# Embedding squares summed in bursts of four tiles, and pool input columns accumulated onto banks that ScalarE has seeded

## The chip, the cores and the metric

The kernel runs on one core of a Trainium2 chip. The time is that of one execution on the device, in microseconds (us): before the change a median of 2209.13 over 3 runs (2203.75 to 2210.25). One further execution was profiled; it took 2208.09, and its span from the first to the last instruction is 2206.3. All times in the rows below are microseconds from the start of that span.

The engines are TensorE (PE; its weight loads are listed apart as PEld), VectorE (DVE), ScalarE (ACT), GpSimd (POOL) and SyncE (SP), which issues the DMAs.

## The reference, cut to what matters

```python
def trunk_layer(x, p, S0, buf0, start, w_in, w_pool, ...):      # two layers; 512 prompt + 64 sample tokens
    h = rmsnorm(x, pre_g)
    proj = h @ w_in
    u, gp, q, k, v, gr = jnp.split(proj, SPLITS, axis=-1)
    pool_y, buf_new = pool_mixer(u, buf0, start, w_pool, pool_scale)   # causal means of 2, 4, 8, 16 tokens
    pool_y = pool_y * jax.nn.silu(gp)
    ret_y, S_new = retention(q, k, v, S0, start)
    ret_y = head_rmsnorm(ret_y).reshape(B, L, RET_WIDTH) * jax.nn.silu(gr)
    mix = jnp.concatenate([pool_y, ret_y], axis=-1) @ w_out
    x = x + rmsnorm(mix, post_g)
    ple = rmsnorm(p @ w_ple, ple_g)
    gate = jax.nn.sigmoid(x @ w_ple_gate + b_ple_gate)
    return x + gate * ple, S_new, buf_new
```

`pool_mixer` takes four groups of 256 channels: a windowed sum over tokens, divided by the count, minus `u`, times a 256 x 256 matrix. The gain `pre_g` is multiplied into the input before the product with `w_in`; the root of the norm, one number per token, is multiplied in afterwards (`rB`).

## The kernel before

All activations are held transposed: 128 channels on the partitions, 576 tokens (512 prompt, 64 sample) along the free dimension, in two halves of 288 columns (`half`, `HN`), because one PSUM bank takes one half. An fp32 product is made of three passes: each operand is split into a rounded upper part and a rest (`split`, L88: a cast on ACT, a subtraction on DVE), and upper x upper, upper x rest and rest x upper are added up in PSUM.

Each of the two layers runs through these stages.

- `in_first` (L386): the first half of the input channels times `w_in`, by a scheme with seven products in place of eight (`unit`, L234). The partial results go to DRAM (`proj_dram`).
- `in_phase` (L469): the second half. `columns(pr)` (L472) gives two tiles of 128 output channels. For each it loads the partial result into a buffer of the tag `part` (L478), splits the weights, and calls `gemm` (L129): 8 x 3 passes x 2 halves = 48 matmuls of 288 columns into two banks of the tag `acc`. Then DVE adds bank and partial result into the `part` tile (L484). Four heads come first (queries, keys, values and a gate, eight columns each), then four pool groups, g = 3, 2, 1, 0.
- `pool_group(g)` (L656): two input columns. Each is multiplied by `rB` into a tile `e` of the tag `d` (L669, L670), and its sample part into a tile `es` of the tag `u` (L672), which is first filled from DRAM (L663). Two scans per column (L680) give the windowed sums, the second of the tiles `tmp` and `es`. L682 to L689 make the means, and the result is split into two `u` tiles. Then come two gate columns (L500, L501), and for each half of the group's output the product with `w_pool` into `po` banks (L696) and the product with the gate into a tile `y` of the tag `d` (L700, L704). Between the groups, `operands(..., tag="part")` prepares what `out_phase` needs.
- `out_phase` (L721): the output projection by units, its norm (`rsqrt` of `rM`, L749, with two squares into `tmp` at L748), then the per-layer embedding: for 16 tiles, L761 to L770, a `gemm` of 12 matmuls, the square of both banks on ACT (L766, L316), their copy into a `part` tile (L768), the sum of the square over channels by four small matmuls with a tile of ones (`token_sums`, L290 and L292; each shows as two instructions), and the store. All 16 sums add up in one `po` bank. Then the gate product, which starts from the mixed result and the norm `rM`.

The order of the instructions on each engine is made by a planner ahead of time: it goes through the program, and places each instruction where its own simulation finds the engine free and the inputs there. An instruction that first writes a tile also waits for a buffer of the tile's tag. The numbers of buffers per tag are in `BUFS` (L44): `part` 4, `tmp` 4, `d` 4, `u` 6, `g` 2; there are 4 `acc` banks (L121), 2 `po` (L124) and 2 `pb` (L127).

Of the kernel before, what the change touches and what calls it, by code (L numbers as in the profile page):

```python
# [11 lines left out]
ALU = mybir.AluOpType  # L12
# [4 lines left out]
KT = 16  # L17
# [16 lines left out]
def half(ap, h):  # L34
    return ap[:, h * HN:(h + 1) * HN]
# [3 lines left out]
def decoder_kernel(ctx: ExitStack, tc: tile.TileContext, a, decay8):  # L39
# [86 lines left out]
    def bank(shape):  # L126
        return ps.tile(list(shape), F32, tag="pb", name="pb", bufs=2)  # L127

    def gemm(w, xs, new=acc_tile, by_half=False):  # L129
        acc = [new()[:, :HN] for _ in range(2)]  # L130
        n = len(w)
        for hs in ((0,), (1,)) if by_half else ((0, 1),):
            for i, ((wh, wl), (xh, xl)) in enumerate(zip(w, xs)):
                for passno, (u, v) in enumerate(((wh, xh), (wh, xl), (wl, xh))):
                    for h in hs:
                        nc.tensor.matmul(  # L136
                            acc[h], u, v[:, h * HN:(h + 1) * HN],
                            start=(i == 0 and passno == 0), stop=(i == n - 1 and passno == 2),
                        )
        return acc  # L140

# [148 lines left out]
    def token_sums(sums, src, start, stop):  # L290
        for q in range(4):
            nc.tensor.matmul(sums[32 * q:32 * q + 32], ones, src[:, q * QN:(q + 1) * QN], start=start, stop=stop)  # L292

    def rsqrt(out, srcs, n, sums=None):
        if sums is None:
            sums = mix_tile()[:, :QN]
            for i, src in enumerate(srcs):
                token_sums(sums, src, i == 0, i == len(srcs) - 1)
        v, t, r = (w[:, i * QN:(i + 1) * QN] for w in (tmp(),) for i in range(3))
        nc.vector.tensor_scalar(v, sums, 1.0 / n, EPS, op0=ALU.mult, op1=ALU.add)  # L300
        nc.vector.tensor_scalar(r.bitcast(I32), v.bitcast(I32), 1, None, op0=ALU.logical_shift_right)
        nc.vector.tensor_scalar(r.bitcast(I32), r.bitcast(I32), -1.0, float(0x5F3759DF), op0=ALU.mult, op1=ALU.add)
        for _ in range(3):
            nc.vector.scalar_tensor_tensor(out=t, in0=r, scalar=-0.5, in1=r, op0=ALU.mult, op1=ALU.mult)
            nc.vector.tensor_tensor(out=t, in0=t, in1=v, op=ALU.mult)
            nc.vector.scalar_tensor_tensor(out=r, in0=t, scalar=1.5, in1=r, op0=ALU.add, op1=ALU.mult)
        for h in range(2):
            rows = mix_tile()[:, :HN]
            for q in (2 * h, 2 * h + 1):
                nc.tensor.matmul(rows[:, (q % 2) * QN:(q % 2 + 1) * QN], pick[:, q], r, start=True, stop=True)  # L310
            nc.scalar.copy(half(out, h), rows)

    def square(out, src):
        if isinstance(src, list):
            for h in range(2):
                nc.scalar.activation(half(out, h), src[h], AF.Square)  # L316
        else:
            nc.scalar.activation(out, src, AF.Square)

# [11 lines left out]
    def load_tables():  # L331
# [6 lines left out]
        consts["kdec_s"] = load_const("kdec_s", [P, NH, NS])  # L338
        consts["mask_s"] = load_const("mask_s", [P, NH, 64])
        consts["invcnt"] = load_const("invcnt", [P, 4, 16])  # L340

    def after_all(ins, others):
        for other in others:
            tc.add_manual_dep(
                ins.ins, other.ins.name, mybir.DependencyInfo(mybir.DependencyClass.Sync, mybir.DependencyReason.DATA),
                reason="one burst",
            )

    def retention_state(l, h, s0_ring, qrep, kst, vst, po_s):
        for bg in range(2):  # L350
# [118 lines left out]
    def in_phase(l, raws, r2, rB, cos, sin):  # L469
        b_ring, st_ring, rot_ring, s0_ring = Ring(0, 12), Ring(12, 4), Ring(16, 8), Ring(24, 4)  # L470

        def columns(pr):  # L472
            keys = [("in2", p) for p in pairs] + [("out", 0, 0), ("out", 0, 1)]
            i = keys.index(("in2", pr))
            raw = raws.pop(("in2", pr))
            for c in range(2):
# [2 lines left out]
                w = split_weights(raw, 8 * c, 8)  # L479
                if c == 1:  # L480
                    fetch(l, raws, keys[i + 1:i + 3])
                acc = gemm(w, r2)
                for h in range(2):
                    nc.vector.tensor_tensor(out=half(t, h), in0=acc[h], in1=half(t, h), op=ALU.add)  # L484
# [171 lines left out]
        def pool_group(g):  # L656
# [7 lines left out]
            wh, wl = buf("u", (P, 2, DK), F32R), buf("u", (P, 2, DK), F32R)  # L664
            split(wh, wl, wraw)
            xs = []
            for i, t in enumerate(columns(g)):
                e = buf("d", (P, 16 + NP))
                nc.vector.memset(e[:, :16], 0.0)  # L669
                nc.vector.tensor_tensor(out=e[:, 16:], in0=t[:, :NP], in1=rB[:, :NP], op=ALU.mult)  # L670
                seg = es[:, i, 16:].rearrange("p (b s) -> p b s", s=SEG)
                nc.vector.tensor_tensor(  # L672
                    out=seg[:, :, BUF:], in0=t[:, NP:].rearrange("p (b s) -> p b s", s=NS),
                    in1=rB[:, NP:].rearrange("p (b s) -> p b s", s=NS), op=ALU.mult,
                )
                nc.scalar.copy(npool[:, i, 0], e[:, NP + 1:])
# [44 lines left out]
    def out_phase(l, raws, ops_out):  # L721
# [30 lines left out]
        for k in range(2):  # L752
# [3 lines left out]
            split(hi, lo, t)  # L756
            pp.append((hi, lo))
        sums = mix_tile()[:, :QN]
        for c8 in range(2):
            raw = load_weights(a["w_ple"][l, :, c8 * 8:(c8 + 1) * 8].rearrange("p c k n -> p (c k) n"))  # L760
            w = split_weights(raw, 0, 16)  # L761
            for c in range(8):
                ct = c8 * 8 + c
                acc = gemm(w[2 * c:2 * c + 2], pp)
                t, sq = buf("part"), buf("u")
                square(sq, acc)  # L766
                for i in range(2):
                    nc.scalar.copy(half(t, i), acc[i])  # L768
                token_sums(sums, sq, ct == 0, ct == KT - 1)
                nc.sync.dma_start(out=ple_dram[l][ct], in_=t)  # L770

        def residual(first):
            def xs(k):
# [192 lines left out]
```

## Time and profile before

| | us |
|---|---|
| median of 3 runs | 2209.13 |
| lowest, highest | 2203.75, 2210.25 |
| the profiled execution | 2208.09 |
| its span | 2206.3 |

The page of the profile gives the busy time of each engine over the span, the costliest groups of instructions by line, and the chain of work that ended last. Matmuls are pipelined, so a matmul's own duration (some 290 ns) is longer than the distance from one start to the next (some 130 ns for 288 columns); stretches of many matmuls tell more than single durations. A line can be that of a helper: L316 is any square of two banks, L318 any other square, L91 any rest of a split. Numbers in brackets behind a row of a timeline are the engine's idle time before it, and what ended it.

### The profile page before, as it was taken

The page shows a single profiled execution, that of the slowest core. Times are in us where ns is not written, and L with a number is a line of the kernel's source. Part 1 is how long each engine was busy: PE and PEld are TensorE (multiplying, and loading weights), DVE is VectorE, ACT ScalarE, POOL GpSimd, SP SyncE. Part 2 cuts the span into 40 slices and gives each one's busy share as a digit, 9 for nine tenths or more (in the row PEclk, how much of TensorE's full clock was granted, in tenths as well). Part 3 has the DMA queues.
Part 4 walks back from the last instruction along what each step waited for, and adds up shares of the span by engine and source line. Part 5 has one row for each costly group of instructions (what it writes and reads, how often), then busy time and mean ns, then how long its engine had stood idle before and what let it go on. Part 6 is the DMA issues. An engine that isn't in the chain of part 4 may idle for free.

```text
span 2206.3 us, 42552 instructions
## 1 busy us (share of the span) xinstructions
PE 2179.7 (99%) x16692; PEld 2138.2 (97%) x16692; DVE 1724.1 (78%) x3186; ACT 1059.0 (48%) x2097; POOL 89.5 (4%) x65
## 2 busy tenths in 40 slices
PE   8999999999999999999999999999999999999998
PEld 8999999999999999899999999999999999998998
DVE  8788766767689998888877786666676899988865
ACT  5465433444334555655455554433343345566532
POOL 2000000000000110000110000000000011100000
PEclk9999999999999999999999999999999999999999
DMA  6454455546453434556644444455554543345554
GB/s 227 146 195 166 155 169 159 174 160 186 152 177 127 136 118 136 196 171 219 201 161 152 166 156 152 161 178 173 159 171 152 171 147 123 112 144 192 175 197 151
DMA packets 138729, 361.98 MB, mean 164 GB/s; under 512 B 14496, under 2 KB 52896, under 8 KB 117664
## 3 DMA queue, kind: packets, MB, share of 16 engines
q1 hardware_dynamic: 138528, 359.26, 49.3%
q8 instruction: 131, 2.15, 0.4%
q14 instruction: 70, 0.57, 0.1%
HBM read 273.17 MB, written 86.04 MB: 163 GB/s over the span
## 4 chain that ended last, share of the span: by engine, by line
PE 87%; DVE 5%; DMA 5%; issue 2%; ACT 1%; SPq 0%; POOL 0%; DVEq 0%; ACTq 0%; POOLq 0%
PE acc L136 32%; PE acc L118 12%; PE acc L117 12%; PE acc L116 12%; PE acc L226 4%; DMA x<-ple 3%; PE pb L116 3%; PE pb L117 3%; PE pb L118 3%; PE po L292 1%; PE po L136 1%; DVE wl L91 1%; DVE x L801 1%; PE po L359 1%; PE pb L375 1%
## 5 line engine op out<-in xcount | busy, mean ns | idle before, releaser
L136 PE MATMUL acc<-m,wh 128*128 128x288 f32 x3584 | 657.0, 297 | 4.0 <-DVE part L484 4.0
L90 ACT CAST wh<-raw 128x512 fp32r<-128x512 f32 x567 | 350.3, 619 | 530.3 <-PE acc L136 288.1
L117 PE MATMUL acc<-m,wh 128*128 128x288 f32 x1944 | 572.3, 295 | 0.0
L116 PE MATMUL acc<-m,wh 128*128 128x288 f32 x1944 | 570.4, 295 | 0.8 <-ACT m L249 0.8
L118 PE MATMUL acc<-m,wl 128*128 128x288 f32 x1944 | 566.3, 295 | 1.2 <-DVE wl L91 1.2
L136 PEld LDWEIGHTS acc<-m,wh 128*128 128x128 f32 x3584 | 534.7, 189 | 11.7 <-issue 8.4
L91 DVE TENSOR_TENSOR wl<-raw,wh 128x512 fp32r<-128x512 f32 x567 | 395.7, 700 | 130.1 <-ACT wh L90 122.7
L136 PE MATMUL acc<-m,wl 128*128 128x288 f32 x1792 | 396.9, 296 | 0.0
L116 PEld LDWEIGHTS acc<-m,wh 128*128 128x128 f32 x1944 | 364.3, 188 | 2.0 <-ACT m L249 1.5
L117 PEld LDWEIGHTS acc<-m,wh 128*128 128x128 f32 x1944 | 364.8, 188 | 0.0
L118 PEld LDWEIGHTS acc<-m,wl 128*128 128x128 f32 x1944 | 362.3, 188 | 2.1 <-DVE wl L91 2.1
L90 ACT CAST wh<-S 128x512 fp32r<-128x512 f32 x356 | 220.6, 620 | 252.8 <-PE acc L117 146.1
L136 PEld LDWEIGHTS acc<-m,wl 128*128 128x128 f32 x1792 | 292.6, 189 | 1.9 <-issue 1.4
L91 DVE TENSOR_TENSOR wl<-S,wh 128x512 fp32r<-128x512 f32 x356 | 250.8, 706 | 24.6 <-ACT wh L90 23.2
L239 POOL TENSOR_TENSOR S<-raw 128x512 f32<-128x512 f32 x45 | 71.4, 1588 | 1923.6 <-DMA raw<-in_w_out 664.9
L484 DVE TENSOR_TENSOR part<-acc,part 128x288 f32<-128x288 f32 x192 | 79.3, 451 | 69.8 <-PE acc L136 67.3
L239 DVE TENSOR_TENSOR S<-raw 128x512 f32<-128x512 f32 x133 | 94.8, 712 | 10.8 <-DMA raw<-in_w_in 7.4
L116 PE MATMUL pb<-m,wh 128*128 128x288 f32 x324 | 95.3, 294 | 0.6 <-ACT wh L90 0.6
L117 PE MATMUL pb<-m,wh 128*128 128x288 f32 x324 | 95.5, 295 | 0.0
L118 PE MATMUL pb<-m,wl 128*128 128x288 f32 x324 | 95.0, 293 | 0.0
L249 ACT COPY d<-acc 128x288 f32<-128x288 f32 x228 | 86.1, 394 | 0.0
L254 DVE TENSOR_TENSOR d<-d,acc 128x288 f32<-128x288 f32 x114 | 51.3, 450 | 39.6 <-PE acc L118 39.3
(264 smaller groups left out, 3289.6 us busy)
## 6 DMA issues: line engine op xcount, KB each, us to landing
raw<-in_w_in SPq DMA_DIRECT2D x95, 1024.0 KB, 5.3
raw<-in_w_out SPq DMA_DIRECT2D x32, 1024.0 KB, 4.8
raw<-in_w_gate SPq DMA_DIRECT2D x32, 1024.0 KB, 5.3
proj<-d SPq DMA_DIRECT2D x96, 288.0 KB, 2.2
part<-proj SPq DMA_DIRECT2D x96, 288.0 KB, 3.0
m<-in_state_ret SPq DMA_DIRECT2D x64, 256.0 KB, 3.3
out_new_ret_s<-m SPq DMA_DIRECT2D x64, 256.0 KB, 3.2
x<-m SPq DMA_DIRECT2D x48, 288.0 KB, 3.4
```

The costliest lines, as they stand in the source:

```text
L90: nc.scalar.copy(hi, src)
L91: return nc.vector.tensor_tensor(out=lo, in0=src, in1=hi.bitcast(F32), op=ALU.subtract)
L116: nc.tensor.matmul(out, wh, xh, start=start, stop=False, **kw)
L117: nc.tensor.matmul(out, wh, xl, start=False, stop=False, **kw)
L118: nc.tensor.matmul(out, wl, xh, start=False, stop=stop, **kw)
L136: nc.tensor.matmul(acc[h], u, v[:, h * HN:(h + 1) * HN], start=(i == 0 and passno == 0), stop=(i == n - 1 and passno == 2),)
L226: nc.tensor.matmul(acc[h], w[:, j], xs[h][passno == 1], start=(i == 0 and j == 0 and passno == 0), stop=(i == 1 and j == 3 and passno == 2),)
L239: eng.tensor_tensor(out=s, in0=x, in1=y, op=op)
L249: ops["tail_act"] = nc.scalar.copy(dst, src)
L254: return nc.vector.tensor_tensor(out=dst, in0=dst, in1=src, op=ALU.add)
L292: nc.tensor.matmul(sums[32 * q:32 * q + 32], ones, src[:, q * QN:(q + 1) * QN], start=start, stop=stop)
L484: nc.vector.tensor_tensor(out=half(t, h), in0=acc[h], in1=half(t, h), op=ALU.add)
```

## The change

Two changes are made at once.

First, the sums of the embedding's squares. `token_sums` was called for each of the 16 tiles. Now the squares are kept in a list, and when four are there, `together` issues the matmuls of all four; its first one waits in addition for the last square of the four (`last_square`, `after_all`). The square tiles, before in buffers of `u`, now take the tags tmp, tmp, tmp, tmp, g, g, u, u in turn.

Second, the pool group's input columns. `columns(g, seeded=True)` has ScalarE copy the two halves of the partial result from the `part` tile into the two `acc` banks before the first matmul (`seed`), and the matmuls add to it (`start` is false from the first one on). The DVE addition of L484 falls away for these 2 columns of 4 groups in 2 layers, and the generator hands out the two banks in place of the `part` tile. The product with `rB` reads the banks: it becomes two instructions, 288 and 224 columns wide, and the product for the sample part reads the second bank.

```diff
--- before.py
+++ after.py
@@ -126,16 +126,22 @@
     def bank(shape):
         return ps.tile(list(shape), F32, tag="pb", name="pb", bufs=2)
 
-    def gemm(w, xs, new=acc_tile, by_half=False):
+
+
+    def gemm(w, xs, new=acc_tile, by_half=False, seed=None):
         acc = [new()[:, :HN] for _ in range(2)]
         n = len(w)
+        if seed is not None:
+            for h in range(2):
+                nc.scalar.copy(acc[h], half(seed, h))
         for hs in ((0,), (1,)) if by_half else ((0, 1),):
             for i, ((wh, wl), (xh, xl)) in enumerate(zip(w, xs)):
                 for passno, (u, v) in enumerate(((wh, xh), (wh, xl), (wl, xh))):
                     for h in hs:
                         nc.tensor.matmul(
                             acc[h], u, v[:, h * HN:(h + 1) * HN],
-                            start=(i == 0 and passno == 0), stop=(i == n - 1 and passno == 2),
+                            start=(seed is None and i == 0 and passno == 0), stop=(i == n - 1 and passno == 2),
+                            skip_group_check=seed is not None,
                         )
         return acc
 
@@ -291,6 +297,16 @@
         for q in range(4):
             nc.tensor.matmul(sums[32 * q:32 * q + 32], ones, src[:, q * QN:(q + 1) * QN], start=start, stop=stop)
 
+    def together(sums, srcs, start, stop):
+        for i, src in enumerate(srcs):
+            for q in range(4):
+                mm = nc.tensor.matmul(
+                    sums[32 * q:32 * q + 32], ones, src[:, q * QN:(q + 1) * QN],
+                    start=start and i == 0, stop=stop and i == len(srcs) - 1,
+                )
+                if q == i == 0:
+                    after_all(mm, [last_square[0]])
+
     def rsqrt(out, srcs, n, sums=None):
         if sums is None:
             sums = mix_tile()[:, :QN]
@@ -310,10 +326,19 @@
                 nc.tensor.matmul(rows[:, (q % 2) * QN:(q % 2 + 1) * QN], pick[:, q], r, start=True, stop=True)
             nc.scalar.copy(half(out, h), rows)
 
+    last_square = [None]
+
+    def after_all(ins, others):
+        for other in others:
+            tc.add_manual_dep(
+                ins.ins, other.ins.name, mybir.DependencyInfo(mybir.DependencyClass.Sync, mybir.DependencyReason.DATA),
+                reason="one burst",
+            )
+
     def square(out, src):
         if isinstance(src, list):
             for h in range(2):
-                nc.scalar.activation(half(out, h), src[h], AF.Square)
+                last_square[0] = nc.scalar.activation(half(out, h), src[h], AF.Square)
         else:
             nc.scalar.activation(out, src, AF.Square)
 
@@ -338,13 +363,6 @@
         consts["kdec_s"] = load_const("kdec_s", [P, NH, NS])
         consts["mask_s"] = load_const("mask_s", [P, NH, 64])
         consts["invcnt"] = load_const("invcnt", [P, 4, 16])
-
-    def after_all(ins, others):
-        for other in others:
-            tc.add_manual_dep(
-                ins.ins, other.ins.name, mybir.DependencyInfo(mybir.DependencyClass.Sync, mybir.DependencyReason.DATA),
-                reason="one burst",
-            )
 
     def retention_state(l, h, s0_ring, qrep, kst, vst, po_s):
         for bg in range(2):
@@ -469,7 +487,7 @@
     def in_phase(l, raws, r2, rB, cos, sin):
         b_ring, st_ring, rot_ring, s0_ring = Ring(0, 12), Ring(12, 4), Ring(16, 8), Ring(24, 4)
 
-        def columns(pr):
+        def columns(pr, seeded=False):
             keys = [("in2", p) for p in pairs] + [("out", 0, 0), ("out", 0, 1)]
             i = keys.index(("in2", pr))
             raw = raws.pop(("in2", pr))
@@ -479,6 +497,9 @@
                 w = split_weights(raw, 8 * c, 8)
                 if c == 1:
                     fetch(l, raws, keys[i + 1:i + 3])
+                if seeded:
+                    yield gemm(w, r2, seed=t)
+                    continue
                 acc = gemm(w, r2)
                 for h in range(2):
                     nc.vector.tensor_tensor(out=half(t, h), in0=acc[h], in1=half(t, h), op=ALU.add)
@@ -664,13 +685,14 @@
             wh, wl = buf("u", (P, 2, DK), F32R), buf("u", (P, 2, DK), F32R)
             split(wh, wl, wraw)
             xs = []
-            for i, t in enumerate(columns(g)):
+            for i, acc in enumerate(columns(g, seeded=True)):
                 e = buf("d", (P, 16 + NP))
                 nc.vector.memset(e[:, :16], 0.0)
-                nc.vector.tensor_tensor(out=e[:, 16:], in0=t[:, :NP], in1=rB[:, :NP], op=ALU.mult)
+                nc.vector.tensor_tensor(out=e[:, 16:16 + HN], in0=acc[0], in1=rB[:, :HN], op=ALU.mult)
+                nc.vector.tensor_tensor(out=e[:, 16 + HN:], in0=acc[1][:, :NP - HN], in1=rB[:, HN:NP], op=ALU.mult)
                 seg = es[:, i, 16:].rearrange("p (b s) -> p b s", s=SEG)
                 nc.vector.tensor_tensor(
-                    out=seg[:, :, BUF:], in0=t[:, NP:].rearrange("p (b s) -> p b s", s=NS),
+                    out=seg[:, :, BUF:], in0=acc[1][:, NP - HN:].rearrange("p (b s) -> p b s", s=NS),
                     in1=rB[:, NP:].rearrange("p (b s) -> p b s", s=NS), op=ALU.mult,
                 )
                 nc.scalar.copy(npool[:, i, 0], e[:, NP + 1:])
@@ -756,18 +778,22 @@
             split(hi, lo, t)
             pp.append((hi, lo))
         sums = mix_tile()[:, :QN]
+        squares = []
         for c8 in range(2):
             raw = load_weights(a["w_ple"][l, :, c8 * 8:(c8 + 1) * 8].rearrange("p c k n -> p (c k) n"))
             w = split_weights(raw, 0, 16)
             for c in range(8):
                 ct = c8 * 8 + c
                 acc = gemm(w[2 * c:2 * c + 2], pp)
-                t, sq = buf("part"), buf("u")
+                t, sq = buf("part"), buf(("tmp", "tmp", "tmp", "tmp", "g", "g", "u", "u")[ct % 8])
                 square(sq, acc)
                 for i in range(2):
                     nc.scalar.copy(half(t, i), acc[i])
-                token_sums(sums, sq, ct == 0, ct == KT - 1)
                 nc.sync.dma_start(out=ple_dram[l][ct], in_=t)
+                squares.append(sq)
+                if len(squares) == 4:
+                    together(sums, squares, ct == 3, ct == KT - 1)
+                    squares = []
 
         def residual(first):
             def xs(k):
```

## Rows read from the trace of the kernel before

**Rows 1.** The page: busy time of the engines; two of its groups.
```profile
PE 2179.7 (99%) x16692; PEld 2138.2 (97%) x16692; DVE 1724.1 (78%) x3186; ACT 1059.0 (48%) x2097; POOL 89.5 (4%) x65
...
L484 DVE TENSOR_TENSOR part<-acc,part 128x288 f32<-128x288 f32 x192 | 79.3, 451 | 69.8 <-PE acc L136 67.3
...
L249 ACT COPY d<-acc 128x288 f32<-128x288 f32 x228 | 86.1, 394 | 0.0
```
**Rows 2.** The chain of waits, 876 to 894 us: start, us, what.
```profile
876.11 6.58 PE acc L136 x48
...
883.67 1.92 PE po L292 x56
...
887.37 0.38 PE po L292 x8
...
889.54 0.37 PE po L292 x4
...
892.63 0.98 PE acc L136 x6
```
**Rows 3.** Line L292 in the first layer's embedding: count, duration ns, first and last start.
```profile
L292 PE MATMUL po<-u,ones x128: 286/286/310, 883.7 to 912.4; 128*32 128x144 f32 x128
```
**Rows 4.** Timeline of PE behind the pool waits: start, us, what [idle before].
```profile
639.88 0.50 PE L136 MATMUL acc<-m,wh 128*128 128x288 f32 x2 [2.01 <-DVE part L484]
...
1733.98 0.50 PE L136 MATMUL acc<-m,wh 128*128 128x288 f32 x2 [2.01 <-DVE part L484]
```
**Rows 5.** Timeline of ACT, head 3's normaliser.
```profile
608.82 0.89 ACT L311 COPY tmp<-po 128x288 f32<-128x288 f32 x2 [0.28 <-PE po L310]
```
**Rows 6.** Timeline of DVE, first layer's pool stage, 565 to 633 us.
```profile
569.13 0.82 DVE L484 TENSOR_TENSOR part<-acc,part 128x288 f32<-128x288 f32 x2
...
570.47 0.68 DVE L670 TENSOR_TENSOR d<-part,long 128x512 f32<-128x512 f32 x1
...
584.89 0.32 DVE L672 TENSOR_TENSOR u<-part,long 128x64 f32<-128x64 f32 x2
...
598.01 0.82 DVE L484 TENSOR_TENSOR part<-acc,part 128x288 f32<-128x288 f32 x2 [1.05 <-PE acc L136]
...
608.06 0.82 DVE L484 TENSOR_TENSOR part<-acc,part 128x288 f32<-128x288 f32 x2 [1.94 <-PE acc L136]
...
609.40 1.22 DVE L680 TENSOR_TENSOR_SCAN tmp<-d 128x512 f32<-128x512 f32 x1
...
621.83 0.75 DVE L91 TENSOR_TENSOR u<-tmp,u 128x576 fp32r<-128x576 f32 x1
...
629.96 0.95 DVE L700 SCALAR_TENSOR_TENSOR d<-po,c_pool_scale,g 128x288 f32<-128x288 f32 x2
630.42 0.07 DVE L669 MEMSET d<- 128x16 f32 x1
630.83 1.29 DVE L670 TENSOR_TENSOR d<-part,long 128x512 f32<-128x512 f32 x2
```
**Rows 7.** Timeline of ACT, 866 to 874 us.
```profile
866.85 0.41 ACT L316 ACTIVATE u<-acc 128x288 f32<-128x288 f32 x1 [0.87 <-PE acc L136]
...
872.84 1.26 ACT L318 ACTIVATE tmp<-m 128x576 f32<-128x576 f32 x2
```
**Rows 8.** Timeline of DVE, 876 us.
```profile
876.18 0.31 DVE L300 TENSOR_SCALAR tmp<-po 128x144 f32<-128x144 f32 x1 [2.62 <-PE po L292]
```
**Rows 9.** Windows: length, busy us of PE, PEld, DVE, ACT, POOL, clock, DMA.
```profile
884.00:906.00 22.00, 22.00 (x208) 16.50 (x200) 18.01 (x29) 18.52 (x53) 0.00 (x0) 1.00 0.80 269
```
**Rows 10.** The chain of waits, 608 to 620 us.
```profile
608.29 0.98 PE po L310 x8
609.27 9.99 PE acc L136 x75
```
**Rows 11.** Timeline of DVE, second layer's pool stage.
```profile
1702.16 0.82 DVE L484 TENSOR_TENSOR part<-acc,part 128x288 f32<-128x288 f32 x2 [1.94 <-PE acc L136]
...
1724.52 0.07 DVE L669 MEMSET d<- 128x16 f32 x1
```
**Rows 12.** Windows behind the two waits of rows 4.
```profile
639.90:643.30 3.40, 3.40 (x26) 3.40 (x27) 3.40 (x11) 1.30 (x3) 0.00 (x0) 1.00 0.89 286
1734.60:1738.00 3.40, 3.40 (x17) 3.40 (x16) 3.40 (x8) 0.94 (x2) 0.00 (x0) 0.50 0.88 319
```

## The prediction, made before the changed kernel was run

> **What bounds the kernel now.** I read the page's engine shares first: TensorE (PE) is busy 99% of the span, DVE 78%, ACT 48% [rows 1]. So nothing that is taken from DVE or ACT shortens the kernel by itself; a saving must come out of PE's work, and each wait of PE is a loss. Then I read the chain of waits and the timelines of the two stages that the diff touches: the per-layer embedding, 865 to 912 us, and the pool stage, 565 to 690 us. Both come again in the second layer, some 1095 us later.
>
> In the embedding stage PE is never idle, but it changes its work often. A run of 48 matmuls of 288 columns takes 6.58 us, 0.137 each [rows 2]. Between them stand the token sums, 128 instructions in a layer [rows 3], in 18 bursts: one of 56 in 1.92 us, one of 8 in 0.38, sixteen of 4 in 0.37 [rows 2]. A burst of 4 costs as much as one of 8: what is paid is the change of work. The six matmuls behind such a burst take 0.98 us [rows 2] instead of 6 x 0.137 = 0.82, so another 0.16 belongs to it.
>
> In the pool stage PE has one wait of 2.0 us in each layer, ended by the DVE addition at L484 [rows 4].
>
> **Part one, the bursts.** Before: (1.92 + 0.16) + (0.38 + 0.16) + 16 x (0.37 + 0.16) = 11.1 us in a layer. One more instruction inside a burst costs (1.92 - 0.38) / 48 = 0.032 us, so the change of work costs 0.38 + 0.16 - 8 x 0.032 = 0.28. After: four bursts of 32, 128 x 0.032 + 4 x 0.28 = 5.2. That is 5.9 us less PE work per layer.
>
> Two things eat from it. First, the squares of tiles 0 to 3 now take "tmp" buffers. The trace shows that buffers of one tag are given out in program order, the next not before the one ahead has been written: the scan of the first pool group stands on DVE at 609.40, behind the copy of the normaliser into the "tmp" tile ahead of it, at 608.82 [rows 5, 6], although its input was there after 570.47 [rows 6]. In the embedding stage two squares of the projection's last tiles (872.84) and the scratch of its normaliser (876.18) stand ahead of tile 0's square in that tag; before, that square used "u" and ran at 866.85, ahead of both [rows 7, 8]. Now tiles 0 and 1 keep every bank that the last units leave until 872.84, and tile 3 waits for the normaliser's scratch. PE loses filler work. Bounds: nothing, if the last unit simply moves up into the hole; two and a half tiles of 12 x 0.137, 4 us, if it can't. I take 1, since only a short piece of a unit is left then. Second, ACT: it was busy 18.5 of the 22 us from 884 to 906, DVE 18.0 [rows 9]. PE had 22 us of work there and would have some 16, so the stage runs into ACT at about 18.5: 2.4 of the 5.9 are lost. This leaves 5.9 - 1 - 2.4 = 2.5 us per layer, bounds 5.9 and (with 4 for 1) -0.5.
>
> **Part two, the seeded banks.** Removed: 32 additions of 451 ns on DVE, 14.4 us. Added: 32 copies on ACT, nearest row 394 ns, 12.6 us [rows 1], and one more DVE instruction for each of 16 columns. The idle shares of ACT (52%) and DVE (22%) hide this. A seed needs its "part" load a whole product (48 x 0.137 = 6.6 us) earlier than the addition did. The loads of the second group were late because "part" was held until L672 at 584.89 [rows 6]; a seed lets it go earlier, so I put this at nothing (without that, up to 6 us a layer).
>
> The price is how long banks are held. Before, the additions read them at once (598.01 and 608.06 for the two columns of the second group), and L670, the product with rB, read the SBUF copy only at 630.83 [rows 6]. After, L670 itself reads the bank. There are four "acc" banks, and one column takes two. L670 can't come earlier: its output is a "d" tile, and by the order above it stands behind the two y tiles of the group before; its memset, 630.42, stands right behind the second y, 629.96 [rows 6]. That y needs the first group's w_pool products, these its scans, and these the "tmp" tile of head 3's normaliser at 608.82 [rows 5]. So from the end of the second group's columns at 608.06 until the first of its banks is read, no gate column can start. Before, PE used this time: 75 matmuls on "acc" in 9.99 us behind the picks of 608.29 [rows 10], and more later. This work now has no bank.
>
> How long? DVE works without a break from 609.40 to the second split at 621.83 [rows 6], and nearly all of it stays. The two additions (0.82) and a wait of 0.44 among it go: the operands are ready at 621.3. Then come half a w_pool product (0.8), its first read (0.5), the second product (1.6; both use the two "po" banks), two reads by L700 (1.0) and the first half of L670 (0.45): a bank is free at 625.7. PE ends the picks at 608.29 + 0.98 = 609.3 [rows 10] and has 24 w_pool matmuls (3.2 us) meanwhile: 625.7 - 609.3 - 3.2 = 13.2 us lost. Bounds: 10.2, if 3 us of weight splits and head 3's products leave DVE's way; 18.8, if nothing moves up and the bank comes free at 631.3, as L670's first half ended (631.3 - 609.3 - 3.2). In the second layer the distance is the same, 1702.16 to 1724.52 [rows 11] against 608.06 to 630.42, so this counts twice. For the later groups the y come while PE still has two gate columns (13 us) to do: they cost nothing, and these columns are the cover.
>
> **The clock.** After the 2.0 us wait in the second layer the granted clock was 0.50, the lower level, from 1734.6 to 1738.0: 17 matmuls in 3.40 us. The same wait in the first layer left it at 1.00, and the like stretch there holds 26 [rows 12]: 9 matmuls, 1.2 us lost. I count 1.2 behind each long wait (bounds 0 and 2.4).
> The Trainium skill, "TensorE: Matmul & The Clock Gate", section "HAM oscillation — how this bites in real kernels", says that a PE which waits too long between products starts each next one cold. [...]
>
> **The sum.** Pool stage: 2 x (13.2 + 1.2) = +28.8. The two present waits of 2.0 us end with an addition that falls away, with the slow clock behind one: -5.2. Bursts: -5.0. Together +18.6 on the profiled execution's 2208.1 gives 2226.7; the median of the runs lies 1.0 above that execution, so 2228.
>
> **Rivals.** (a) *The banks are not held.* If the planner lets L670 of the second group run right behind its columns, as in the first group (addition 569.13, L670 570.47 [rows 6]), no bank is missing: 2209 - 5.2 - (5 to 11.8) = 2192 to 2199, say 2195, faster. For it: the first group, and a DVE with less to do. Against it: L669 right behind the y tile in both layers [rows 6, 11]. It decides by whether the second group's L669 comes before the first group's last L700.
> (b) *A short hold.* If normaliser and scans move up by some 9 us, since PE and DVE are emptier, 4 us of wait stay: 2 x (4 + 1.2) - 5.2 - 5 = 0, so 2209. Against it: the DVE rows stand back to back.
> (c) *The bursts cost too.* If the banks of the embedding are held as long as bounded above, the bursts give +1 instead of -5: 2234; with the hold of 18.8 as well, 2245.
> (d) *The bursts don't form*, because the planner still sends sums apart. The burst of 56 [rows 2] shows that sums which are ready together go together, so it gets no chance of its own; it would take away the 5, 2233.
> The Trainium skill, "Perfetto Trace Analysis", section "Optimizing Tensor Performance", asks that groups of matmuls rotate through banks, so that the evacuation of one overlaps the next. The change gives that up where a bank waits for L670; by this rule it is slower, and [rows 6] shows by how much the reading would come late.
>
> **How the numbers follow.** The forecast as summed 0.65, (a) 0.15, (b) 0.07, (c) 0.13. The forecast's own ends are 2 x 10.2 - 5.2 - 11.8 = +3.4, 2212, and the 2245 of (c). To leave out no more than 2 in 10 the range goes down to 2200, into the gap before (a), and up to 2248. A measurement tells 0.3%, 6.6 us, from no change: faster 0.15, same 0.07, slower 0.78.
>
> **What would show it.** Right: PE without work for some 10 us behind the second pool group's second column in both layers, ended by DVE at L670; the clock at 0.50 behind it; four bursts of token sums of about 1 us per layer; no wait for the addition at 639 and 1733. Wrong: L670 of the second group within a few us of its columns; waits of more than 4 us in the embedding stage; a wait for a seed whose load lands late.

## The result, and the profile after

The kernel after took 2224.05 us (median of 4 runs, 2222.52 to 2226.47), the kernel before, beside it, 2208.97. The ratio is 1.0075, 95% interval 1.0061 to 1.0088: slower by 15 us. One further execution was profiled: 2226.47, with a span of 2224.7 against 2206.3.

First the engines on the page of the kernel after (busy us, share of the span, instructions), then two groups of its DVE and ACT lists (busy, mean ns of one, idle before), which answer to [rows 1]:

```profile
PE 2180.9 (98%) x16692; PEld 2146.1 (96%) x16692; DVE 1719.1 (77%) x3170; ACT 1071.6 (48%) x2129; POOL 86.7 (4%) x65
...
L505 DVE TENSOR_TENSOR part<-acc,part 128x288 f32<-128x288 f32 x160 | 66.0, 452 | 68.9 <-PE acc L141 66.1 <-DMA out_new_ret_s<-m 2.2
...
L136 ACT COPY acc<-part 128x288 f32<-128x288 f32 x32 | 12.3, 402 | 3.4 <-DVE part L505 3.4
```

32 additions are gone from DVE and 32 copies of 402 ns have come to ACT, as the prediction priced them. The loss is not to be seen here: PE has the same 16692 instructions, and its busy time is even 1.2 us longer. It shows in the waits and in the clock of the pool stage.

The PE waits of the first layer's pool stage, 575 to 660 us (us in total, times, longest); before, the 2.0 us of [rows 4] stood here alone:

```profile
PE po L377 <- DMA m<-in_state_ret: 5.4, 1, 5.4
PE po L141 <- DVE u L91: 3.1, 2, 2.9
PE po L141 <- ACT u L90: 1.1, 1, 1.1
PE acc L141 <- DVE d L691: 0.5, 1, 0.5
PE po L141 <- DVE d L722: 0.4, 1, 0.4
```

And windows of the kernel after (length, busy us and count of PE, PEld, DVE, ACT, POOL; granted clock; DMA share; GB/s), which answer to [rows 12]:

```profile
588.00:594.80 6.80, 4.93 (x29) 3.76 (x30) 2.44 (x7) 2.23 (x6) 0.00 (x0) 0.50 0.52 161
594.80:622.20 27.40, 24.72 (x199) 23.86 (x198) 20.07 (x46) 10.82 (x22) 0.00 (x0) 1.00 0.39 117
622.20:635.80 13.60, 11.11 (x41) 10.07 (x42) 12.44 (x30) 5.60 (x11) 0.00 (x0) 0.50 0.78 265
1690.50:1697.30 6.80, 4.92 (x29) 3.65 (x30) 2.44 (x7) 2.23 (x6) 0.00 (x0) 0.50 0.63 201
1724.70:1734.90 10.20, 7.69 (x27) 6.64 (x28) 9.69 (x25) 4.65 (x9) 0.00 (x0) 0.50 0.77 258
```

So there are two holes in each layer, each with a stretch at the lower clock (0.50) that begins in it: one of 5.4 us in front of the state product of head 3 (L377), which was not forecast, and the forecast one, whose rows follow. It begins when PE runs out of products on `acc` behind the picks of head 3, and ends when DVE reads the first bank. Timeline of PE (idle before, and what ended it), then of DVE:

```profile
613.72 1.14 PE L326 MATMUL po<-tmp,pick 128*128 128x144 f32 x8
...
618.56 0.42 PE L141 MATMUL acc<-m,wl 128*128 128x288 f32 x2
620.11 0.53 PE L141 MATMUL po<-u 128*128 128x288 f32 x2 [1.13 <-ACT u L90]
623.51 1.81 PE L141 MATMUL po<-u 128*128 128x288 f32 x6 [2.87 <-DVE u L91]
625.52 1.33 PE L141 MATMUL po<-u 128*128 128x288 f32 x4 [0.20 <-DVE u L91]
627.30 3.25 PE L141 MATMUL po<-u 128*128 128x288 f32 x12 [0.45 <-DVE d L722]
631.08 0.85 PE L141 MATMUL acc<-m,wh 128*128 128x288 f32 x2 [0.53 <-DVE d L691]
```
```profile
630.13 0.51 DVE L722 SCALAR_TENSOR_TENSOR d<-po,c_pool_scale,g 128x288 f32<-128x288 f32 x1
630.58 0.44 DVE L691 TENSOR_TENSOR d<-acc,long 128x288 f32<-128x288 f32 x1
630.60 0.07 DVE L690 MEMSET d<- 128x16 f32 x1
...
631.95 0.48 DVE L722 SCALAR_TENSOR_TENSOR d<-po,c_pool_scale,g 128x288 f32<-128x288 f32 x1
```

This is the chain of [rows 6] with the bank at its end: the product with `rB` (now L691) stands right behind the first half of the second y tile (now L722, 630.13). The second half of that y, ahead of L670 before, now comes behind the products of both columns, at 631.95. So the next tile of a tag needs only the first write of the one ahead of it.

To put a price on each stage I counted the columns that PE's matmuls had done by each time of the kernel before, and looked up when the other kernel had done as many. By how much that distance grows in a stage is what the stage costs (us, one profiled execution of each kernel; the embedding includes the hold of its first tiles). Where nothing was changed the distance still drifts by 1 to 2 us (in the kernel after it is +2.1 ahead of the first pool stage), so differences of that size say little:

| kernel | pool, layer 1 | embedding 1 | pool, layer 2 | embedding 2 |
|---|---|---|---|---|
| after | +14.7 | -3.0 | +10.1 | -3.2 |
| bursts | +0.6 | -2.0 | -1.3 | -3.5 |
| seeds | +11.5 | 0.0 | +9.5 | 0.0 |

The two embeddings give back 6.2 us, the two pool stages cost 24.8.

### The profile page after: what moved, and what is told of

Same layout as the page of the kernel before. It is cut to its first block, busy times and chain, and to the rows that moved or that the text cites. A ratio compares the mean times of both kernels' runs of the same rounds, so it can differ in the third digit from the quotient of the medians.

```text
span 2224.7 us, 42566 instructions
## 1 busy us (share of the span) xinstructions
PE 2180.9 (98%) x16692; PEld 2146.1 (96%) x16692; DVE 1719.1 (77%) x3170; ACT 1071.6 (48%) x2129; POOL 86.7 (4%) x65
## 4 chain that ended last, share of the span: by engine, by line
PE 84%; DMA 7%; DVE 5%; ACT 2%; issue 1%; SPq 0%; POOL 0%; ACTq 0%; DVEq 0%; POOLq 0%
PE acc L141 28%; PE acc L117 13%; PE acc L116 13%; PE acc L118 13%; PE acc L232 4%; DMA x<-ple 3%; PE pb L117 3%; PE pb L116 3%; PE pb L118 3%; DMA out_new_ret_s<-m 1%; DMA x<-m 1%; PE po L141 1%; PE po L377 1%; DMA ple<-part 1%; DVE x L827 1%
## 5 line engine op out<-in xcount | busy, mean ns | idle before, releaser
L91 DVE TENSOR_TENSOR wl<-raw,wh 128x512 fp32r<-128x512 f32 x567 | 405.6, 716 | 145.6 <-ACT wh L90 136.4
L505 DVE TENSOR_TENSOR part<-acc,part 128x288 f32<-128x288 f32 x160 | 66.0, 452 | 68.9 <-PE acc L141 66.1
```

The lines of the kernel that those rows point to most:

```text
L91: return nc.vector.tensor_tensor(out=lo, in0=src, in1=hi.bitcast(F32), op=ALU.subtract)
```

## The experiments

Line numbers are those of each kernel; they lie within four of the kernel after (the product with `rB`, L691 there, is L694 in `hold` and `hold_free`). Ratios are to runs of the kernel before on the same chip. Theory: the pool loses because the seeded banks are held until L691, and the bursts gain. Rivals: the seed itself is the price; another reader or buffer holds the banks.

### Each half alone: bursts and seeds

`bursts` is the kernel after with the pool of before, `seeds` the kernel after with the embedding of before.

> The changed kernel with its pool undone: the embedding's bursts alone. If the bursts are the part that gains and the seeded pool the part that loses, this comes out 5 to 7 us under the kernel before (about 2203), the embedding about 3.3 us shorter in each layer, and layer 1's pool as it was. If the bursts bring nothing by themselves, or pay in tmp buffers (sum tiles held from the first square of a burst to its last), it stands at 2209 or above, and with the kernel after in common would be the slow embedding.

> The changed kernel with its embedding undone: seeded pool columns alone. By the theory that the pool loses by held banks it is slower than the kernel after by what the bursts gain: about 2230 (+21), with both holes in the first group of each layer's pool (5 us in front of the state product, 9 to 12 us behind the picks of head 3). If the pool's loss needs the bursts (another order of the whole program), it comes out near 2209.

Measured: `bursts` 2199.11, ratio 0.9967 (0.9955 to 0.9980), `seeds` 2226.27, 1.0089 (1.0074 to 1.0104). The halves have opposite signs, as expected, and the table above shows them by stage. In `seeds` both holes are there in both layers. Of waits above 0.5 us, `bursts` has only the old one of 2.0 us for the addition in each pool stage.

### Bursts of two: pairs

```diff
-                if len(squares) == 4:
-                    together(sums, squares, ct == 3, ct == KT - 1)
+                if len(squares) == 2:
+                    together(sums, squares, ct == 1, ct == KT - 1)
```

> The kernel bursts with bursts of two squares for four. By the terms of the prediction each change of work on PE costs 0.28 us, and this has 4 bursts more in a layer, so 8 changes more: 2.2 us a layer, 4.5 in all, 2203 to 2204 against 2199. If the gain of bursts is not in the number of changes, but in that no product waits for its square any more, pairs have it too: within 1 us of bursts.

Measured: 2199.55, ratio 0.9972 (0.9961 to 0.9983): as fast as `bursts`. The expectation counted each burst as two changes; by the prediction's sum, 0.28 for a burst, four more are 1.1 us a layer, so the two branches lay closer than it says. The price of a change of work is not refuted, and the rows show what balances it. Bursts of four, kernel `bursts`, PE in the first layer's embedding:

```profile
876.25 0.53 PE L141 MATMUL acc<-d,wh 128*128 128x288 f32 x2 [0.95 <-ACT part L790]
...
883.37 1.19 PE L303 MATMUL po<-tmp,ones 128*32 128x144 f32 x32 [1.10 <-ACT tmp L341]
...
903.26 0.53 PE L141 MATMUL acc<-d,wh 128*128 128x288 f32 x2 [1.55 <-ACT part L790]
```

Bursts of two, kernel `pairs`, the same stage:

```profile
882.19 0.70 PE L303 MATMUL po<-tmp,ones 128*32 128x144 f32 x16
883.29 0.70 PE L303 MATMUL po<-tmp,ones 128*32 128x144 f32 x16 [0.41 <-ACT tmp L341]
888.09 0.70 PE L303 MATMUL po<-g,ones 128*32 128x144 f32 x16
```

A burst of 32 takes 1.19 us, one of 16 takes 0.70, so two of 16 cost 0.21 more than one of 32. The pairs pay that, but wait 0.41 us for their first squares where the fours wait 1.10, and don't have the wait of 1.55 for ACT, which `bursts` has in the first layer only. ACT is busy 18.1 us (fours) and 19.3 us (pairs) of the 22 from 881 to 903; that fewer changes on PE buy nothing more because ACT is that close is argued, not shown.

### The banks held, without a seed: hold

```diff
-                    yield gemm(w, r2, seed=t)
+                    acc = gemm(w, r2)
+                    for h in range(2):
+                        nc.vector.tensor_tensor(out=acc[h], in0=acc[h], in1=half(t, h), op=ALU.add)
+                    yield acc
```

> No seeds: the pool's products start on fresh banks, DVE adds the part tile into the bank in place, and the products with rB read the bank, which so stays held as in the kernel after. If holding the banks is the whole loss, this is about as slow as the kernel after: 2218 to 2228. If the seed is the loss, about 2200 to 2206.

Measured: 2214.99, ratio 1.0034 (1.0021 to 1.0047), pool stages +8.0 and +5.1. Against `bursts` (0.9967) holding the banks costs 0.0067, 15 us. That is most of the seeded pool's loss (0.0108 from `bursts` to the kernel after, 24 us) but not all: I had expected 2218 or more. The window 575 to 660 us of the kernels `bursts` and `hold`, in this order, shows it as a count of matmuls and a clock:

```profile
575.00:660.00 85.00, 82.68 (x645) 81.36 (x644) 66.21 (x150) 32.17 (x62) 0.11 (x1) 1.00 0.57 182
```
```profile
575.00:660.00 85.00, 77.56 (x576) 75.22 (x575) 68.91 (x159) 32.30 (x64) 0.00 (x0) 0.94 0.54 178
```

69 matmuls fewer in the same 85 us. The hole before the state product is not in `hold`; the other is, with the same row order on DVE at its end:

```profile
624.87 0.51 DVE L725 SCALAR_TENSOR_TENSOR d<-po,c_pool_scale,g 128x288 f32<-128x288 f32 x1
625.32 0.44 DVE L694 TENSOR_TENSOR d<-acc,long 128x288 f32<-128x288 f32 x1
625.33 0.07 DVE L693 MEMSET d<- 128x16 f32 x1
```

### Freeing the readers: ygate, ygate_es, hold_free

`ygate` is the kernel after with the first edit below, `ygate_es` with both, and `hold_free` is `hold` with both.

```diff
-                y = buf("d")
+                y = gate
```
```diff
-            es = buf("u", (P, 2, 16 + NB * SEG))
+            es = buf("e2", (P, 2, 16 + NB * SEG))      # two buffers
```

> The kernel after, with the gated values y written in place of the gate tile instead of into a d buffer, so that the buffers of the pool's columns e wait for no earlier y. If the d order is what holds the seeded banks, the product with rB runs right behind the last matmul of its bank and the 9 to 12 us hole goes: 2200 to 2212. If the banks are held by the second reader (es, the sample columns) or by the number of banks as such, it stays at 2220 or above.

Measured: 2226.50, ratio 1.0091 (1.0077 to 1.0105). The product with `rB` now runs at once, and still the hole is there, 15 us later. Kernel `ygate`: PE, then DVE and SP:

```profile
639.88 2.12 PE L141 MATMUL po<-u 128*128 128x288 f32 x6 [6.37 <-ACT u L90]
```
```profile
619.20 0.45 DVE L691 TENSOR_TENSOR d<-acc,long 128x288 f32<-128x288 f32 x1
...
637.12 0.35 DVE L694 TENSOR_TENSOR u<-acc,long 128x64 f32<-128x64 f32 x2
```
```profile
633.43 0.39 SPq L684 DMA_DIRECT2D u<-in_state_pool  x1
```

Now the second reader of the upper banks is late, the sample product, which is L694 here. Its tile `es` takes one of the `u` buffers; its load goes out at 633.43, L694 runs at 637.12, and behind it come the scan of `es`, the mean and the split for which the `w_pool` product on PE waits until 639.88. The expectation's second branch was right, so `ygate_es`.

> The kernel after with both buffers freed on which its readers of a held bank wait: y in place of the gate tile, so that the d buffers wait for no y, and the state columns es in two buffers of their own instead of in the u buffers, which wait for the group before. In ygate the hole had moved from 619-631 to 633-644 us, in front of the sample product that reads the upper bank and needs es. If the two readers' buffers are the whole hold, the hole goes in both layers: 2203 to 2210, with 5 to 8 us a layer left if the state loads come late again. If it only moves once more (to the gates or the pool's own products), 2215 or above.

Measured: 2223.63, ratio 1.0071 (1.0054 to 1.0089). With both readers free the hole moved once more, and its last piece names a new cause. Waits of PE, kernel `ygate_es`, 575 to 660 us:

```profile
PE acc L141 <- ACT acc L136: 4.3, 1, 4.3
PE po L141 <- DVE g L722: 3.6, 1, 3.6
PE po L141 <- DVE u L91: 1.5, 1, 1.5
```

Now the products wait for the seed (L136). So two things limit the seeded pool, and freeing one shows the other. The same two edits without seeds tell whether the hold is then gone:

> The run hold (no seeds, the sum added into the bank, which is held until its products with rB) with the buffers of both readers of the bank freed: y in place of the gate tile and es in two buffers of its own. If those two waits are the whole price of holding a bank, the pool's 9 us in each layer go and this is the kernel bursts again: 2198 to 2204. If the banks' number or another wait (y, now in the gate's two tiles) limits it as well, 2208 or above.

Measured: 2195.43, ratio 0.9950 (0.9937 to 0.9964): nearly all of the hold's price is gone. This is the lowest median of the study; its interval overlaps that of `bursts` by 0.0009 and most of that of `evac3` below. The window of `hold_free`, beside the two above, and its only PE wait of more than 0.3 us there, which is what is left of the hold (PE waits for the product with `rB`; 1.4 us in the second layer):

```profile
575.00:660.00 85.00, 83.64 (x652) 82.02 (x651) 72.18 (x170) 34.03 (x67) 0.00 (x0) 1.00 0.56 185
```
```profile
PE acc L141 <- DVE d L694: 1.1, 1, 1.1
```

It also loses the 2.0 us waits that `bursts` still has. Which of the two buffers does how much without seeds was not run apart, nor was `bursts` with both edits, so what the buffers give by themselves is not known.

### The seed without a hold: evac, evac2, evac3

All three seed the banks and copy them out at once on DVE, so that no bank is held; the products behind read the copy, as in the kernel before. They differ in the tiles: `evac` copies into a second `part` tile, `evac2` into the one that seeded, `evac3` seeds from two tiles of their own (`sd`) and copies into a `part` tile.

```diff
-                t = buf("part")
+                t = buf("sd" if seeded else "part")      # evac3 only
...
-                    yield gemm(w, r2, seed=t)
+                    acc = gemm(w, r2, seed=t)
+                    t = buf("part")                      # t2 in evac; left out in evac2
+                    for h in range(2):
+                        nc.vector.tensor_copy(out=half(t, h), in_=acc[h])
+                    yield t
```

> The kernel after, with the banks seeded as there, but each pair of banks copied out at once by DVE into the part tile and read from that by the later products, as the kernel before reads its sum. If the loss is that the banks wait for the products with rB (which stand behind the d buffers of the group before), both layers lose the 9 to 12 us hole and its slow clock: about 2200 to 2206, or some 5 us per layer more if the late state loads stay. If seeding itself is the price (part tiles' loads ahead of the first product, ScalarE's copies in front of a bank's first matmul), it stays at about 2224.

> Banks seeded as in the kernel after, and copied out at once into the very part tile that seeded them, so a column has one part tile and no bank is held, as in the kernel before. The run evac, which took a second part tile for each column, lost its time at another place (633 to 645 us). If seeding costs nothing and only parking the sum matters, this is the kernel bursts again: 2198 to 2204. If seeding itself costs (its load and ScalarE's copy now stand ahead of the products, where the addition stood behind them), it stays above 2212.

> As evac and evac2 (seeded, copied out at once, no bank held), with two tiles of their own for the seeds, so that a seed's load waits for no part tile. In evac2 the load of a seed was issued 2.5 to 6 us ahead of the first product and PE waited 3.2 us for ScalarE's copy. If it is the lack of a free tile that makes seeding dear, this is bursts again: 2198 to 2206. If ScalarE's copies or the order of the program cost it, 2212 or above.

Measured: `evac` 2222.75, ratio 1.0074 (1.0061 to 1.0088); `evac2` 2219.48, 1.0053 (1.0035 to 1.0070); `evac3` 2196.92, 0.9959 (0.9946 to 0.9972). The first two fell on the side of "seeding itself", against my theory that only the hold costs. What it is in seeding is read from `evac2`, SP, ACT and PE:

```profile
631.92 0.33 SPq L496 DMA_DIRECT2D part<-proj  x1
```
```profile
635.18 0.74 ACT L136 COPY acc<-part 128x288 f32<-128x288 f32 x2 [2.38 <-DMA part<-proj]
```
```profile
635.64 0.53 PE L141 MATMUL acc<-m,wh 128*128 128x288 f32 x2 [3.23 <-ACT acc L136]
```

The load, 3 us from its issue to the copy, stands in front of the first product; in the kernel before it stood in front of the addition, with a whole product between. The load itself was issued late, 2.9 us after SyncE was free for it, because its `part` tile was still read by a sample product on DVE. Such waits for the seed are 3.5 of the 8.0 us that PE waits in this pool stage and 7.0 of 13.7 in the second layer's; the others were not followed. Two tiles more take nearly all of them away: the window of `evac3` holds the most matmuls of all, and PE waits for nothing in it.

```profile
575.00:660.00 85.00, 84.98 (x663) 83.61 (x662) 68.93 (x152) 37.13 (x76) 1.75 (x1) 1.00 0.59 196
```

`evac` and `evac3` differ in nothing but the tag of the seed's tile. So ScalarE's copies cost nothing that can be seen, the missing tiles do.

### Everything freed: seed_free

The kernel after with `sd`, `y = gate` and `es` in one buffer of its own.

> The change with all three waits taken away: seeds in two tiles of their own, y in place of the gate tile, es in a buffer of its own. Banks are still seeded by ScalarE and read by the products. If buffers are all that stands against the seeded pool, about as fast as bursts or a little faster (DVE has 16 additions less in a layer): 2196 to 2204. If each bank pair in use takes the room that the next column's products had in before, 2208 or above.

Measured: 2201.09, ratio 0.9983 (0.9971 to 0.9994). The seeded design is healed too, though not faster than `bursts`. What is left stands mostly in the first layer (pool +3.4 and -2.3), a wait of 3.27 us before the state product (1.79 in the second layer):

```profile
589.29 1.94 PE L377 MATMUL po<-m,u 128*32 128x256 f32 x16 [3.27 <-issue]
```

### The first hole: storep

In the kernel before, the second pair of state stores of head 3 (L377 there) is issued ahead of a raw weight load; after, that load goes first. SP of the kernel before, then of the kernel after, and the DMA issues of the kernel after at 570 to 590 us (KB each, median us from issue to landing):

```profile
572.42 1.02 SPq L377 DMA_DIRECT2D out_new_ret_s<-m  x2
573.67 0.35 SPq L102 DMA_DIRECT2D raw<-in_w_in  x1
```
```profile
575.58 0.42 SPq L102 DMA_DIRECT2D raw<-in_w_in  x1
576.09 0.90 SPq L395 DMA_DIRECT2D out_new_ret_s<-m  x2
585.42 1.13 SPq L372 DMA_DIRECT2D m<-in_state_ret  x2
...
out_new_ret_s<-m SPq DMA_DIRECT2D x4, 256.0 KB, 5.8
raw<-in_w_in SPq DMA_DIRECT2D x1, 1024.0 KB, 9.1
```

The next states (L372) take the buffers of the stored ones, so they wait 8.4 us for the stores, and PE waits for them: this is the 5.4 us of L377. (The median of 5.8 mixes two stores ahead of the load, 2.2 and 2.3 us, with two behind it, 9.3 and 9.5.) The experiment gives these stores to another engine:

```diff
-                    nc.sync.dma_start(out=a["new_ret_s"][...], in_=s0)
+                    nc.gpsimd.dma_start(out=a["new_ret_s"][...], in_=s0)
```

> The kernel after with the state stores issued by GpSimd instead of SyncE, so that they don't stand behind a raw weight load in SP's queue. If that load ahead of the stores is why the next states come late, the 5 us gaps at 584 and 1687 us and their slow clock (6.8 us at half clock) go: 8 to 16 us off, about 2208 to 2216. If the late states were hidden by what the second hole takes anyway (a later chain ends at the same time), it gains less than 4: 2220 or above.

Measured: 2217.61, ratio 1.0047 (1.0030 to 1.0064): 0.0028, some 6 us, less than the kernel after, in both layers (pool +10.3 and +7.2). That lies between the two branches of the expectation, and the two intervals overlap by 0.0003. The hole shrank from 5.42 to 2.84 us and didn't close:

```profile
585.80 1.93 PE L377 MATMUL po<-m,u 128*32 128x256 f32 x16 [2.84 <-DMA m<-in_state_ret]
```
```profile
574.60 1.46 POOL L395 DMA_DIRECT2D out_new_ret_s<-m  x2 [2.29 <-DVE m L394]
```

These two stores, issued at 574.60 and 575.34, landed at 581.36 and 582.08, behind the weight load (573.84 to 580.05), although another engine had issued them. The first two, at 570.62 and 571.58 with no weight load under way, took 2.7 us. The packets of the second pair began to move only at 579.13, 4.5 us after the issue, when the load was nearly through; those of the first pair began 1.3 us after theirs. So the place in SyncE's order is not all of it: here a store behind the load came late on another queue as well (7.1 and 6.9 us in the second layer), and what kept it back was not shown.

In the first layer the load goes first in every kernel that both seeds the banks and reads them (the kernel after, `seeds`, `ygate`, `ygate_es`, `seed_free`), and in none that does only one of the two (`hold`, `hold_free`, the three `evac`) or neither (`bursts`). Why the planner does so was not settled. The order alone does not fix the wait of the state product: it is 4.0 to 5.4 us in three of the five, 3.3 in `seed_free` and 0.8 in `ygate_es`.

## Why the prediction was right, point by point

**Direction and size.** 2228 was forecast, 2224 measured. The forecast's mechanism is there in both layers, but the agreement in size is luck: a hole of 14.2 us was left out, the forecast one came out 8.9 us smaller, and the gains 5.3 us larger. These sums are for the profiled execution, the slowest of four (2226.47); by the medians the kernel is 15.1 us slower, where 18.6 was forecast.

**The bursts.** Forecast 5.9 us less on PE, 1 lost to the early `tmp` tiles and 2.4 to ACT, so 2.5 per layer; measured 3.0 and 3.2. Four bursts at 1.12 from start to start and some 0.16 more in the products around each are 5.1 us of PE work against the forecast 5.2. The losses came out smaller than the forecast 3.4: in the kernel after PE waits 1.10 us for the first burst's squares and 0.95 and 0.48 for ACT's copies, 2.5 together, and 2.2 in the second layer. Which of these waits belongs to which of the two terms is not shown. With the gain of 3.0 and 3.2 that makes some 5.5 us less work. So the step held, with the losses taken 1 us too large.

**The seed's late load, "nothing".** This step failed, in two ways. In the kernel after the loads come early, as said (565.28 for the second group). But the planner's new order puts a weight load ahead of the state stores: 5.42 us of idle time, and 29 matmuls in 4.93 us at the lower clock (0.50). At the full clock they would take 2.9 (16 at 1.07, as the state product took in `hold`, and 13 x 0.137): 7.5 us in the first layer, by the same count 6.7 in the second. The prediction went through the queues for the seed's own load and not for what else would change places on SP. And once no bank is held, the seed's load does come late (`evac2`, 3.5 us of waits in one layer and 7.0 in the other), because a `part` tile has to come free first; the upper bound of 6 us a layer that the prediction named in brackets was the right size.

**How long the bank is held.** Forecast 17.4 us from the picks to the free bank (625.7 - 608.3); measured 631.08 - 613.72 = 17.4. The chain through scans and `w_pool` products held as well, and so did the distance in the second layer (1733.60 - 1716.21 = 17.4). The product with `rB` came behind half of the second y and not behind the whole of it.

**What the hold costs.** Forecast 13.2 us of idle time and 1.2 of slow clock; measured, in the first layer, 5.2 (1.13 + 2.87 + 0.20 + 0.45 + 0.53) and 5.5 (41 matmuls in 11.11 us where 41 x 0.137 = 5.6 would do). Two sizes were off. PE had another 31 products on `acc`, 4.1 us, behind the picks. And the clock fell to its lower level while the 24 `w_pool` products ran between the waits, so that work which was to fill the hole took twice as long. The prediction counted 3.4 us at the lower clock, with 1.2 lost and bounds of 0 and 2.4; there were 13.6 and 10.2, with 5.5 and 4.0 lost, and another 6.8 with the first hole. So the idle time lies below its bound of 10.2 and the clock above its own. In all some 14 of 34 us lost in the two pool stages are clock, not waiting.

**The waits for the addition.** Forecast -5.2; the pool stages gave back some 9 (34.1 of holes and clock against 24.8 net). The two waits of 2.0 us are gone, and the later groups get shorter by 1.4 to 1.9 us, which I had not counted; 1.0 more is a wait that the kernel before already had at its state product in the second layer. The later groups cost nothing, as forecast.

**The sum.** Holes and clock +34.1, of which the forecast place has 19.9 (forecast 28.8) and the unforeseen one 14.2; gains of the pool -9.3, which is what the table leaves; bursts -6.2. That is 18.6; the rest of the program sums to -0.2 (+2.1 ahead of the first pool stage, -1.3 and -1.0 behind the two embeddings), which makes the 18.4 between the two spans.

**The rivals.** (a), banks not held, was priced at 2195, 0.9937 of the kernel before. `hold_free` comes near that case without seeds: ratio 0.9950, which the 2195.43 shows too favourably, since the kernel before took 2205.89 beside it; with seeds, `seed_free` has 0.9983. The sign that was to decide (a), L669 of the second group ahead of the first group's last L700, did come (630.60 against 631.95, and in the second layer too), although the banks were held: the first half of a y was enough to hold them, so the sign was badly chosen. (b), a short hold with 4 us of wait, is near the 5.2 us measured, but the hold was no shorter (17.4 us); PE had more to do in it. (c) did not happen, the bursts gained, and neither did (d), they formed. Of the two rules named beside the rows: the Trainium skill, "Perfetto Trace Analysis", section "Optimizing Tensor Performance", asks that groups of matmuls rotate through banks; `hold` against `bursts`, 15 us for banks that are read late, agrees. The Trainium skill, "TensorE: Matmul & The Clock Gate", section "HAM oscillation — how this bites in real kernels", says that a PE which waits too long between products starts the next ones cold; the 5.42 us wait in front of L377, with the clock at 0.50 behind it, agrees. The 2.0 us waits don't tell for or against it: in `bursts` the clock behind both stayed at 1.00, in the second layer of the kernel before it fell.

## What to carry to other kernels

A PSUM bank is only as free as the tile that its reader writes: before a product is left in its bank for a later reader, look up which buffers that reader needs and what holds them, for every reader of the bank. Moving an operand from behind a product to in front of it moves its load too, and needs tiles for it; here two tiles were the difference between 2219 and 2197 us. And when an edit changes a planned program, compare the DMA queue's whole order, not only the DMAs that were touched.

## What the runs showed of the hardware

- The lower clock costs on top of the waiting: in the four holes of the kernel after some 14 us, beside some 20 us of waits. In the first hole 6.8 us at half clock came with one wait of 5.4; in the second 13.6 us began in the wait of 2.87 and went on past three of 0.2 to 0.5 with short products between them. The lone 2.0 us wait of the addition left it at 1.00 in both layers of `bursts`, where the second layer of the kernel before fell to 0.50 [rows 12]; what tells these apart was not found.
- A 256 KB store issued by GpSimd still landed behind a 1024 KB load that SyncE had issued 0.8 us ahead: 6.8 us in place of 2.7.
